# Chain products of two heads as one full tile of the matmul array, and the streams of a round called in the order of tile shapes

## The chip, the cores and the metric

The kernel runs on one core of a Trainium2 chip. Five engines run side by side: TensorE (PE in the profile, its weight loads PEld), VectorE (DVE), ScalarE (ACT), GpSimd (POOL) and SyncE (SP, which issues most DMAs). The metric is the device time of one execution in microseconds; of several executions the median counts.

## The reference

One layer of a hybrid encoder over 1024 positions and 16 learned ones, 1024 wide. A normed input goes through one projection to 5920 columns, which feed three branches; their outputs go through an output projection and are added to the input.

```
z = rms_norm(h) @ w_in
o = concat(na_branch(z), gla_branch(z), rwkv7_branch(z)) @ w_out
h = h + o ; out = rms_norm(h)[16:]

# rwkv7_branch: 8 heads of 64, two directions, a state S of 64 x 64 per head and direction
def step(S, (r, w, k, v, a, b)):
    sa = S @ a
    S  = S * w + outer(sa, b) + outer(v, k)
    y  = S @ r
```

The part that matters here is this last recurrence over the positions.

## The kernel before

All matrices with 1024 rows are split into a high and a low part (fp32r), and the projection is the sum of three products (`pj`, 24 of them per chunk of up to 512 columns). The projection is cut into jobs of 128 columns each, held in a feed.

The recurrence is computed in chunks of 64 positions. Four pairs `p` of heads, each in five groups `j` (one of a single chunk, four of four chunks per direction), make 20 units. In a pair, head e = 0 lies on partitions 0 to 63 and head e = 1 on 64 to 127. Each unit passes through these streams, which are Python generators:

- E (`early`): loads, the small products `lo` (128 rows by 128 columns of the array, written 128\*128), the running sums `Sd` (a scan on DVE) and their exponentials `E1f` and `Sd` on ACT.
- L (`late`): the products `g` inside a chunk (64\*128: 64 rows of the array, 128 columns), cut by masks into `NT`, `XR` and `GR`.
- I and J (`invert`): the inverse of a 64 x 64 triangular matrix per head, chunk and direction, by doubling, with products `fps`, `ta`, `tb`, `eps`, `cps` of 64\*64, in fp16.
- R (`rest`): transposes `v` and `t` that make `SV` and `KT`.
- C (`chain`): the recurrence itself, 68 steps, one for each chunk of each direction and pair. A step has three phases with a yield behind each. Phase 1: `c<-SV,XR` (all 128 rows, two products of 64 columns for each direction, one per head), the products `y<-XR,SV` of 64\*64, and `U` = -2 times the first result, on DVE (L848). Phase 2: `c<-U,TT` of 64\*64, copied by ACT (L853) and DVE (L854) into `SV`. Phase 3: `c<-SV,KT` and `y<-GR,SV` (128\*64 each, per head), `SV` of the next step on DVE (L862), and the output `Y` by one ACT copy (L871) or one DVE addition (L874).
- D (`drain`): the norms of finished groups, with head sums `mn` and `vr` of 128\*128.

`run` goes round these generators. In a round each is advanced once, in the order C, L, I, J, R, E, D, and then eight `pj` products are pulled from the feed. A scheduler orders the instructions of each engine by priority and by dependency afterwards, and ties the `pj` to earlier rounds by manual dependencies; each engine executes its list in order.

A product of two fp32 operands is two instructions on PE (a high and a low pass), an fp32r or fp16 product and a transpose are one. When the last unit has left R, the projection jobs that are left are pulled in one piece; then the attention and GLA branches follow, which the change doesn't touch.

Of the kernel before, what the change touches and what calls it, by code (L numbers as in the profile page):

```python
# [7 lines left out]
F32 = mybir.dt.float32  # L8
# [13 lines left out]
ALU = mybir.AluOpType  # L22

D = 1024
T = 1024
NM = 16
L = T + NM
# [3 lines left out]
C = 64  # L31
# [44 lines left out]
def emit(ctx, tc, a, out):  # L76
    nc = tc.nc
    V, S, G = nc.vector, nc.scalar, nc.gpsimd
    PS = bass.MemoryType.PSUM
    half = (slice(0, 64), slice(64, 128))  # L80
# [23 lines left out]
    PE = Tensor()  # L104
# [553 lines left out]
    def late(u, p, j):  # L658
        st = sts[u]
        ns, kn, k, r, vt, v, inc, exc, BK, dec = (st[n] for n in ("ns", "kn", "k", "r", "vt", "v", "inc", "exc", "BK", "dec4"))  # L660
        m = "" if j else "0"
        XR = it.tile([128, 2, ns, 3, C], F32, name="XR" + m, bufs=2 if j else 1)
        for e in range(2):
            es = half[e]
            (G if 0 else V).tensor_tensor(out=XR[es, :, :, 2 * e, :], in0=exc[es], in1=kn[es], op=ALU.mult)
        if j:
            (G if 1 else V).tensor_tensor(out=XR[:, :, :, 1, :], in0=r, in1=inc, op=ALU.mult)
        yield
        NT = it.tile([128, 2, ns, C], F32, name="NT" + m)
        GR = it.tile([128, 2, 2, ns, C], F32, name="GR", bufs=2) if j else None  # L670
        for d in range(2):
            gps = [mps([128, 4, 128], f"g{e}") for e in range(2)]
            nw = 128 if j else C
            for s in range(ns):
                for e in range(2):
                    es = half[e]
                    rhs = XR[es, d, s, e:e + 2, :] if j else XR[es, d, s, 2 * e, :]
                    PE.matmul(gps[e][:, s, 0:nw], lhsT=BK[es, d, s, e:e + 2, :], rhs=rhs, start=True, stop=True)
            mk = 1 if d and j else 0
            for e in range(2):  # L680
                bs, ks = half[e], half[1 - e]
                ac, rc = (C, 0) if e and j else (0, C)
                V.tensor_tensor(out=NT[bs, d], in0=gps[e][bs, 0:ns, ac:ac + C],
                                in1=nmask[bs, None, mk, :].broadcast_to([64, ns, C]), op=ALU.mult)
                V.tensor_tensor(out=XR[ks, d, :, 2 * e, :], in0=gps[e][ks, 0:ns, ac:ac + C],
                                in1=rmask[ks, None, mk, 0:C].broadcast_to([64, ns, C]), op=ALU.mult)
                if j:
                    V.tensor_tensor(out=GR[:, e, d], in0=gps[e][:, 0:ns, rc:rc + C],  # L688
                                    in1=rmask[:, None, mk, C:128].broadcast_to([128, ns, C]), op=ALU.mult)
            yield  # L690
        st.update(XR=XR, GR=GR, NT=NT)

    def rest(u, p, j):
        st = sts[u]
        ns, k, r, vt, v, BK, dec = (st[n] for n in ("ns", "k", "r", "vt", "v", "BK", "dec4"))
        m = "" if j else "0"
        for e in range(2):
            es = half[e]
            bk = BK[es, :, :, e:e + 2, :]
            G.tensor_tensor(out=bk, in0=bk, in1=dec[es, :, :, None, None].broadcast_to([64, 2, ns, 2, C]), op=ALU.mult)  # L700
        SV = it.tile([128, 2, ns, 2, C], F32, name="SV" + m, bufs=2 if j else 1)
        vps = [mps([128, 2, 4, C], f"v{e}") for e in range(2)]
        for d in range(2):
            for s in range(ns):
                i = 1 + ns * d + s
                PE.transpose(out=vps[0][:, d, s, :], in_=vt[0:64, i - 1:i + 1, :], identity=ident[0:64, 0:64])
                PE.transpose(out=vps[1][0:64, d, s, :], in_=vt[64:128, i, :], identity=ident[64:128, 64:128])
        S.copy(SV[64:128, :, :, 0, :], vps[0][64:128, :, 0:ns])
        S.copy(SV[0:64, :, :, 1, :], vps[1][0:64, :, 0:ns])
        if not j:  # L710
            for e in range(2):
                G.memset(SV[half[e], :, :, e, :], 0.0)
        st["SV"] = SV
        yield
        if j:
            if j <= 2:
                bons[p, 5 - j] = bons[p, j] = it.tile([128, 2, 256], F32, name=f"bon{j}", bufs=3 - j)
            bv = bons[p, j]
            flat = lambda t: t.rearrange("p d s c -> p d (s c)")
            if j <= 2:  # L720
                V.scalar_tensor_tensor(out=bv, in0=flat(r), scalar=hcol(28 + p), in1=flat(k), op0=ALU.mult, op1=ALU.mult)
            else:
                V.scalar_tensor_tensor(out=r, in0=r, scalar=hcol(28 + p), in1=k, op0=ALU.mult, op1=ALU.mult)
                G.tensor_tensor(out=bv, in0=bv, in1=flat(r)[:, ::-1], op=ALU.add)
                yield
                ps = head_sums("bn", bv)
                V.tensor_tensor(out=bv, in0=ps, in1=flat(v)[:, ::-1], op=ALU.mult)
                yield
        KT = it.tile([128, 2, 2, ns, C], F32, name="KT" + m, bufs=2 if j else 1)
        tps = [mps([128, 2, 4, C], f"t{e}") for e in range(2)]  # L730
        for d in range(2):
            for s in range(ns):
                for e in range(2):
                    es = half[e]
                    PE.transpose(out=tps[e][:, d, s, :], in_=BK[es, d, s, e:e + 2, :], identity=ident[es, es])
        for e in range(2):
            S.copy(KT[:, e], tps[e][:, :, 0:ns])
        st["KT"] = KT
        yield

# [71 lines left out]
    def chain(u, nu, p, j):  # L812
# [8 lines left out]
        for i in range(ns):  # L821
# [8 lines left out]
                    nx = two(sts[nu]["SV"].rearrange("p d s e c -> p (d s) e c"), 0, 4)  # L830
            cur = two(sv2, i, ns)
            dcur = two(dec, i, ns)
            cps = pq.tile([128, 3, 2, C], F32, name="c")
            for d in range(2):
                for e in range(2):
                    PE.matmul(cps[half[e], 0, d, :], lhsT=XR[:, d, sd[d], 2 * e, :], rhs=SV[:, d, sd[d], e, :], start=True, stop=True)
            if j:
                yps = pq.tile([128, 2, C], F32, name="y")
                for d in range(2):
                    for e in range(2):  # L840
                        PE.matmul(yps[half[e], d, :], lhsT=SV[half[e], d, sd[d], e, :], rhs=XR[half[e], d, sd[d], 1, :],
                                  start=not d, stop=False, skip_group_check=True)
# [6 lines left out]
            yield  # L849
            for d in range(2):  # L850
                for e in range(2):
                    PE.matmul(cps[half[e], 1, d, :], lhsT=TT[half[e], d, sd[d], :], rhs=U[half[e], d, :], start=True, stop=True)
            S.copy(cur[0:64, :, 0, :], cps[0:64, 1])  # L853
            V.tensor_copy(cur[64:128, :, 1, :], cps[64:128, 1])  # L854
            yield
            if not last:
                for d in range(2):
                    for e in range(2):
                        PE.matmul(cps[half[e], 2, d, :], lhsT=KT[:, e, d, sd[d], :], rhs=SV[:, d, sd[d], e, :], start=True, stop=True)
                for e in range(2):  # L860
                    es = half[e]
                    V.tensor_tensor(out=nx[es, :, e, :], in0=cps[es, 2], in1=dS[es], op=ALU.add)  # L862
            if j:
                for d in range(2):
                    for e in range(2):
                        PE.matmul(yps[half[e], d, :], lhsT=SV[:, d, sd[d], e, :], rhs=GR[:, e, d, sd[d], :], start=False, stop=True,
                                  skip_group_check=True)
                q0, q1 = 4 * j - 4 + i, 19 - 4 * j - i
                Yc = chunked(Y)
                if q1 > q0:  # L870
                    S.copy(Yc[:, q0:q1 + 1:q1 - q0], yps)  # L871
                else:
                    yv = Yc[:, q1:q0 + 1:q0 - q1]
                    V.tensor_tensor(out=yv, in0=yps[:, ::-1], in1=yv, op=ALU.add)  # L874
            yield

    def finish(p, j):
# [32 lines left out]
    past = []  # L910

    HPO = {}
    def run(gens, quota):
        kinds = {id(g): k for k, g in zip('CLIJRED', gens)}
        while gens:
            alive, marks = [], []
            for g in gens:
                off = HPO.get(kinds[id(g)], 0)
                if off:
                    with tc.high_priority(off):  # L920
# [4 lines left out]
                    alive.append(g)  # L925
                if seen:
                    marks.append(seen)
            gens = alive
# [630 lines left out]
```

## Time and profile before

| | before |
|---|---|
| median of 3 executions | 1480.39 us (1479.76 to 1481.89) |
| profiled execution: time | 1480.26 us |
| profiled execution: span of the core | 1478.5 us |
| PE busy | 92% of the span |
| DVE, ACT, POOL busy | 60%, 42%, 42% |
| recurrence, first `g` to last `y` | from 123.5 to 978.6 us |

The span is what the trace covers; 1.8 us lie around it. Busy time of PE is from the start of an instruction to its modelled end, and matmuls overlap, so what an instruction really takes from PE is read from the distance of one start to the next.

### The profile page before, as it was taken

Reading aid. Unit: us, or ns where it says so; the run is one execution under the profiler, and the core shown is the slowest. Engines: PE = TensorE matmul, PEld = TensorE weight load, DVE = VectorE, ACT = ScalarE, POOL = GpSimd, SP = SyncE. Lnnn points to the kernel's source line nnn. Section 1 sums busy time; section 2 is a strip of 40 time slices with the busy share of each in tenths; the row PEclk is TensorE's granted clock in tenths of the full one; section 3 lists DMA queues with packets and bytes.
Section 4 is the critical chain, followed back from the end, with each engine's and each line's share of the span. In section 5 each row is a group of like instructions: output and inputs, shape, how many; then the busy total and the mean of one; then the engine's idle time right before and its main releaser. Section 6 shows DMA issues by size and latency. Waiting matters only on the chain. (4 is left out here: it accounts for less than half of the span.)

```text
span 1478.5 us, 36082 instructions
## 1 busy us (share of the span) xinstructions
PE 1356.0 (92%) x14688; PEld 1160.2 (78%) x14688; DVE 893.9 (60%) x1952; ACT 619.0 (42%) x1400; POOL 616.0 (42%) x719
## 2 busy tenths in 40 slices
PE   5888888999899999999999999987999989789997
PEld 4887777877778788788888888776888878678786
DVE  6435455676756565756656564446767576785554
ACT  5324143334533433434334332335475645645333
POOL 6335364464636764657655554321211111210123
PEclk9998999999989999999999999998999989999999
DMA  7665543533433434333433432245342423633232
GB/s 206 143 145 132 132 107 82 129 90 73 110 102 73 120 92 115 88 103 93 107 102 80 103 94 61 64 96 146 87 130 72 127 76 103 227 111 97 95 94 92
DMA packets 184807, 158.90 MB, mean 107 GB/s; under 512 B 19152, under 2 KB 168048, under 8 KB 184640
## 3 DMA queue, kind: packets, MB, share of 16 engines
q1 hardware_dynamic: 119616, 117.12, 26.7%
q0 software_dynamic: 63264, 35.20, 13.0%
q10 hardware_dynamic: 1760, 4.26, 0.8%
q8 instruction: 116, 1.90, 0.5%
q14 instruction: 51, 0.42, 0.1%
HBM read 123.81 MB, written 32.72 MB: 106 GB/s over the span
## 5 line engine op out<-in xcount | busy, mean ns | idle before, releaser
L93 PE MATMUL pj<-hhi,whi 128*128 128x348 f32 (+10 forms) x1088 | 378.5, 348 | 9.9 <-DVE zt L263 7.5
L93 PE MATMUL pj<-hlo,whi 128*128 128x348 f32 (+10 forms) x1088 | 376.4, 346 | 0.0
L93 PE MATMUL pj<-hhi,wlo 128*128 128x348 f32 (+8 forms) x1064 | 367.6, 346 | 3.9 <-POOL wlo L166 3.9
L93 PEld LDWEIGHTS pj<-hhi,whi 128*128 128x128 f32 (+1 forms) x1088 | 212.5, 195 | 24.2 <-issue 9.7
L93 PEld LDWEIGHTS pj<-hhi,wlo 128*128 128x128 f32 x1064 | 209.5, 197 | 14.8 <-POOL wlo L166 4.4
L93 PEld LDWEIGHTS pj<-hlo,whi 128*128 128x128 f32 (+1 forms) x1088 | 212.7, 196 | 10.7 <-issue 0.7
L166 POOL TENSOR_TENSOR wlo<-wraw,whi 128x512 fp32r<-128x512 f32 x94 | 125.4, 1335 | 163.7 <-DMA whi<-in_w_in_dram 57.4
L162 POOL DMA_DIRECT2D whi<-in_w_in_dram x94 | 74.2, 790 | 144.0 <-PE pj L93 121.2
L700 POOL TENSOR_TENSOR BK<-BK,dec 64x1024 f32<-64x1024 f32 (+1 forms) x40 | 68.4, 1709 | 49.5 <-PE g L93 46.0
L846 POOL TENSOR_TENSOR dS<-SV,dec 64x128 f32<-64x128 f32 x128 | 58.9, 460 | 72.0 <-DVE SV L862 66.7
L792 ACT CAST XA<-ta 128x512 f16<-128x512 f32 (+1 forms) x92 | 49.8, 541 | 90.4 <-PE ta L93 87.1
L93 PE MATMUL ops<-hhi,oh 128*128 128x512 f32 x256 | 85.7, 401 | 2.0 <-DVE yv L1330 2.0
L786 DVE TENSOR_TENSOR Fc<-fps,im 128x512 f16<-128x512 f32 (+1 forms) x92 | 58.4, 636 | 46.5 <-PE fps L93 42.5
L93 PE MATMUL g<-XR,BK 64*128 64x128 f32 (+1 forms) x544 | 67.5, 294 | 5.8 <-DVE GR L688 5.8
L93 PEld LDWEIGHTS g<-XR,BK 64*128 64x128 f32 x544 | 53.7, 190 | 16.7 <-issue 12.5
L93 PEld LDWEIGHTS o_ps<-VC,pT 128*128 128x128 f32 (+2 forms) x384 | 53.5, 195 | 14.2 <-DVE pT L1231 7.2
L93 PE MATMUL o_ps<-VC,pT 128*128 128x64 f32 (+2 forms) x384 | 56.8, 272 | 8.0 <-DVE pT L1231 6.8
L257 ACT ACTIVATE zt<-pj,cols 128x347 f32<-128x347 f32 (+1 forms) x42 | 23.0, 549 | 85.5 <-PE pj L93 68.9
L93 PEld LDWEIGHTS ops<-hhi,oh 128*128 128x128 f32 x256 | 48.6, 191 | 13.0 <-DVE yv L1330 2.4
L1330 DVE TENSOR_TENSOR yv<-ops,yv 128x512 f32<-128x512 f32 x48 | 33.0, 688 | 42.3 <-PE ops L93 42.2
L862 DVE TENSOR_TENSOR SV<-c,dS 64x128 f32<-64x128 f32 x128 | 36.6, 286 | 34.8 <-PE c L93 32.5
L1214 ACT ACTIVATE sc<-sc,nm 128x288 f32<-128x288 f32 (+3 forms) x64 | 37.7, 588 | 45.5 <-DVE nm L1212 45.1
(302 smaller groups left out, 3039.2 us busy)
## 6 DMA issues: line engine op xcount, KB each, us to landing
whi<-in_w_in_dram POOLq DMA_DIRECT2D x94, 256.0 KB, 3.9
wraw<-in_w_in_dram SPq DMA_DIRECT2D x94, 256.0 KB
lr<-rwl POOLq DMA_DIRECT2D x32, 256.0 KB, 3.7
rwz<-zt SPq DMA_DIRECT2D x12, 544.0 KB
orr<-oscr SPq DMA_DIRECT2D x96, 64.0 KB
wr<-in_w_out_dram SPq DMA_DIRECT2D x12, 512.0 KB
glz<-zt SPq DMA_DIRECT2D x8, 544.0 KB
k<-rwz SPq DMA_DIRECT2D x32, 128.0 KB
```

The source lines that it names most:

```text
L93: return place(nc.tensor.matmul(*args, **kw))
L162: G.dma_start(out=hi, in_=w_v[:, q:q + 4, c0:c0 + 128])
L166: G.tensor_tensor(out=lo, in0=raw, in1=hi.bitcast(F32), op=ALU.subtract)
L257: S.activation(zt[:, PAD + n0:PAD + n1], ps[:, n0 - lo:n1 - lo], AF.Copy, scale=c1)
L700: G.tensor_tensor(out=bk, in0=bk, in1=dec[es, :, :, None, None].broadcast_to([64, 2, ns, 2, C]), op=ALU.mult)
L786: V.tensor_tensor(out=Fc, in0=fps, in1=mskt(l), op=ALU.mult)
L792: S.copy(A, aps)
L846: G.tensor_tensor(out=dS[es], in0=cur[es, :, e, :], in1=dcur[es, :, None].broadcast_to([64, 2, C]), op=ALU.mult)
L862: V.tensor_tensor(out=nx[es, :, e, :], in0=cps[es, 2], in1=dS[es], op=ALU.add)
L1214: S.activation(sc[:, 0:m], sc[:, 0:m], AF.Exp, bias=nm, accum_out=sm)
L1330: V.tensor_tensor(out=o, in0=ps, in1=o, op=ALU.add)
```

## The change

The two products of a direction that use all 128 rows (one per head, 64 columns each) become one product of 128 columns with both heads' 64 columns moving. Its result is 128 x 128, of which only the two diagonal blocks are read. This holds for `c<-SV,XR`, `c<-SV,KT` and `y<-GR,SV`. For that `XR` and `KT` are stored with the two heads side by side. `U` is now made in two halves, one on DVE and one on ACT (L845 and L846 of the changed kernel); `y<-XR,SV` moves from phase 1 to phase 2; `Y` is written by two copies or two additions instead of one. And the round calls its generators sorted by a rank: E 0, D 1, R 2 at its head sums, C 3 or 4 by its phase, L 5, I 6, J 7, R 8.

```diff
 late:
-            ...out=XR[es, :, :, 2 * e, :], in0=exc[es], in1=kn[es], op=ALU.mult)
+            ...out=XR[es, :, :, e, :], in0=exc[es], in1=kn[es], op=ALU.mult)
-            ...out=XR[:, :, :, 1, :], in0=r, in1=inc, op=ALU.mult)
+            ...out=XR[:, :, :, 2, :], in0=r, in1=inc, op=ALU.mult)
 rest:
+                shape["R"] = 2
                 yield
+                shape["R"] = 8
-        KT = it.tile([128, 2, 2, ns, C], F32, name="KT" + m, bufs=2 if j else 1)
+        KT = it.tile([128, 2, ns, 2, C], F32, name="KT" + m, bufs=2 if j else 1)
 chain:
-            cps = pq.tile([128, 3, 2, C], F32, name="c")
+            cps = pq.tile([128, 6, C], F32, name="c")
+            both = cps[:, 0:4].rearrange("p (d e) c -> p d e c", d=2)
+            own = cps[:, 4:6]
             for d in range(2):
-                for e in range(2):
-                    PE.matmul(cps[half[e], 0, d, :], lhsT=XR[:, d, sd[d], 2 * e, :], rhs=SV[:, d, sd[d], e, :], ...)
-            if j:
-                yps = pq.tile([128, 2, C], F32, name="y")
-                ... y<-XR,SV
+                PE.matmul(both[:, d], lhsT=XR[:, d, sd[d], 0:2, :], rhs=SV[:, d, sd[d]], start=True, stop=True)
-            V.tensor_scalar(out=U, in0=cps[:, 0], scalar1=-2.0, scalar2=None, op0=ALU.mult)
+            V.tensor_scalar(out=U[0:64], in0=both[0:64, :, 0, :], scalar1=-2.0, scalar2=None, op0=ALU.mult)
+            S.mul(U[64:128], both[64:128, :, 1, :], -2.0)
+            shape["C"] = 4
             yield
+            if j:
+                yps = pq.tile([128, 2, 2, C], F32, name="y")
+                ... y<-XR,SV
             ... c<-U,TT and its two copies
+            shape["C"] = 3
             yield
                 for d in range(2):
-                    for e in range(2):
-                        PE.matmul(cps[half[e], 2, d, :], lhsT=KT[:, e, d, sd[d], :], rhs=SV[:, d, sd[d], e, :], ...)
+                    PE.matmul(both[:, d], lhsT=KT[:, d, sd[d]], rhs=SV[:, d, sd[d]], start=True, stop=True)
             if j:
                 for d in range(2):
-                    for e in range(2):
-                        PE.matmul(yps[half[e], d, :], lhsT=SV[:, d, sd[d], e, :], rhs=GR[:, e, d, sd[d], :], ...)
+                    PE.matmul(yps[:, d], lhsT=SV[:, d, sd[d]], rhs=GR[:, :, d, sd[d], :], ...)
-                    S.copy(Yc[:, q0:q1 + 1:q1 - q0], yps)
+                    for e in range(2):
+                        S.copy(Yc[half[e], q0:q1 + 1:q1 - q0], yps[half[e], :, e, :])
 run:
+        rank = {"E": 0, "D": 1, "C": 3, "L": 5, "I": 6, "J": 7, "R": 8}
-            for g in gens:
+            for g in sorted(gens, key=lambda g: shape.get(kinds[id(g)], rank[kinds[id(g)]])):
```

How the lists of the engines change is shown at three places. The first is on PE, phase 3 of a step in pair 2 (the trace of before shows it at 641 us). Before:

```order
L93 LDWEIGHTS Fc
L93 MATMUL tb<-XU,Fc 64x64
L93 MATMUL y<-GR,SV 64x64
L93 MATMUL pj<-hhi,whi 128x346
L93 MATMUL c<-SV,KT 64x64 x4
L93 MATMUL y<-GR,SV 64x64 x3
L93 MATMUL pj<-hlo,whi 128x346
```

And the same phase of the same step in the change:

```order
L93 LDWEIGHTS Fc
L93 MATMUL tb<-XU,Fc 64x64
L93 MATMUL c<-SV,KT 128x128 x2
L93 MATMUL y<-GR,SV 128x128 x2
L93 MATMUL pj<-hlo,whi 128x346
```

Four products of `c` are two, and four of `y`, of which one stood alone ahead of a `pj`, are two behind `c`; between `tb` and the last `pj` the tile shape changes once instead of four times. The second place is on PE too, phase 1 of a later step of that pair (663 us in the trace of before; the number behind `g` is a buffer's). Before:

```order
L93 MATMUL pj<-hhi,wlo 128x342
L93 MATMUL pj<-hhi,whi 128x342
L93 MATMUL c<-SV,XR 64x64 x4
L93 MATMUL y<-XR,SV 64x64 x4
L93 MATMUL g_10070<-XR,BK 128x128
L93 MATMUL g_10071<-XR,BK 128x128
```

In the change:

```order
L93 MATMUL pj<-hhi,whi 128x342
L93 MATMUL pj<-hlo,whi 128x342
L93 MATMUL c<-SV,XR 128x128 x2
L93 MATMUL y<-XR,SV 64x64 x4
L93 MATMUL g_9910<-XR,BK 128x128
```

The `y` products still follow `c`, since the scheduler moves them up; the change of shape between `pj` and `c` is gone, those from `c` to `y` and from `y` to `g` stay. The third place is on ACT, at the exponentials of stream E for the same unit of pair 2. Before:

```order
L853 COPY SV<-c 64x2x64
L792 CAST XA<-ta 128x512
L793 CAST XU<-tb 128x512
L643 ACTIVATE E1f<-Sd 128x2x4x64
L646 ACTIVATE Sd<-Sd 128x512
L325 COPY zt<-pj 128x348
L792 CAST XA<-ta 128x512
```

In the change:

```order
L794 CAST XA<-ta 128x512
L795 CAST XU<-tb 128x512
L643 ACTIVATE E1f<-Sd 128x2x4x64
L646 ACTIVATE Sd<-Sd 128x512
L846 ACTIVATE U<-c 64x128
L325 COPY zt<-pj 128x348
L794 CAST XA<-ta 128x512
```

The new half of `U` stands on ACT right behind the exponentials, where a copy out of PSUM for the projection stood.

## Rows read from the trace of the kernel before

**Rows 1.** The page, part 1: busy time, share of the span, instructions.

```profile
PE 1356.0 (92%) x14688; PEld 1160.2 (78%) x14688; DVE 893.9 (60%) x1952; ACT 619.0 (42%) x1400; POOL 616.0 (42%) x719
```

**Rows 2.** Recurrence in windows: length, busy (count) of PE, PEld, DVE, ACT, POOL; PEclk, DMA.

```profile
123.50:300.00 176.50, 157.95 (x1919) 137.71 (x1920) 102.75 (x197) 65.47 (x143) 89.80 (x103) 0.94 0.43 108
300.00:640.00 340.00, 319.92 (x4593) 270.95 (x4593) 217.00 (x429) 136.69 (x291) 199.25 (x237) 0.94 0.39 98
640.00:880.00 240.00, 237.19 (x3597) 199.79 (x3595) 144.18 (x299) 93.62 (x205) 143.67 (x165) 1.00 0.38 97
880.00:978.60 98.60, 95.93 (x1173) 80.86 (x1173) 49.47 (x111) 30.00 (x65) 39.49 (x51) 0.98 0.28 66
sum 855.10, PE 810.99 PEld 689.32 DVE 513.41 ACT 325.78 POOL 472.20; mean PE 202.75 PEld 172.33 DVE 128.35 ACT 81.45 POOL 118.05
```

**Rows 3.** Timeline of PE, phase 1: start us, us, what, rows\*columns, form, count.

```profile
663.09 0.32 PE L93 MATMUL pj<-hhi,wlo 128*128 128x342 f32 x1
663.25 0.32 PE L93 MATMUL pj<-hhi,whi 128*128 128x342 f32 x1
663.49 0.45 PE L93 MATMUL c<-SV,XR 128*64 128x64 f32 x8
663.87 0.45 PE L93 MATMUL y<-XR,SV 64*64 64x64 f32 x8
664.25 0.49 PE L93 MATMUL g<-XR,BK 64*128 64x128 f32 x4
664.67 0.44 PE L93 MATMUL cps<-XU,Fc 64*64 64x64 f16 x16
665.04 0.42 PE L93 MATMUL pj<-hlo,whi 128*128 128x342 f32 x1
665.31 0.32 PE L93 MATMUL pj<-hhi,wlo 128*128 128x342 f32 x1
```

**Rows 4.** Timeline of PE, phase 3 of an earlier step.

```profile
640.89 0.33 PE L93 MATMUL y<-GR,SV 128*64 128x64 f32 x2
641.15 0.43 PE L93 MATMUL pj<-hhi,whi 128*128 128x346 f32 x1
641.51 0.45 PE L93 MATMUL c<-SV,KT 128*64 128x64 f32 x8
641.79 0.40 PE L93 MATMUL y<-GR,SV 128*64 128x64 f32 x6
642.12 0.43 PE L93 MATMUL pj<-hlo,whi 128*128 128x346 f32 x1
```

**Rows 5.** Timeline of PE, a longer burst of stream L.

```profile
666.49 0.94 PE L93 MATMUL g<-XR,BK 64*128 64x128 f32 x12
667.36 0.42 PE L93 MATMUL pj<-hhi,wlo 128*128 128x340 f32 x1
```

**Rows 6.** Timeline of PE in the GLA branch: products of one tile at a time.

```profile
1047.97 1.16 PE L93 MATMUL dps<-Vs,kdT 64*128 64x128 f32 x8
1049.06 0.66 PE L93 MATMUL o_ps<-VC,pT 96*128 96x64 f32 x4
```

**Rows 7.** Groups by form: count, busy us, mean ns, idle us before and releaser.

```profile
L93 PE MATMUL c<-SV,XR 128*64 128x64 f32 x544 | 32.1, 237 | 0.0
L93 PE MATMUL c<-SV,KT 128*64 128x64 f32 x512 | 32.0, 240 | 9.8 <-DVE SV L854 9.8
L93 PE MATMUL y<-GR,SV 128*64 128x64 f32 x512 | 45.1, 234 | 1.8 <-DVE SV L854 1.6 <-ACT SV L853 0.2
```

**Rows 8.** Waits of ACT: us in total, times, longest us.

```profile
ACT E1f L643 <- DVE Sd L634: 32.0, 14, 4.9
```

**Rows 9.** Instructions of single tiles: duration in ns, least, median, most.

```profile
L848 DVE TENSOR_SCALAR U<-c x68: 273/291/293, 131.6 to 974.9; 128x128 f32<-128x128 f32 x68
L871 ACT COPY Y<-y x32: 248/265/289, 227.8 to 886.7; 128x128 f32<-128x128 f32 x32
L874 DVE TENSOR_TENSOR Y<-y,Y x32: 272/291/293, 327.2 to 978.8; 128x128 f32<-128x128 f32 x32
```

More of the change, by code (lines that the diff above doesn't have):

```diff
@@ L664, in late @@
             es = half[e]
[L665 removed]
+            (G if 0 else V).tensor_tensor(out=XR[es, :, :, e, :], in0=exc[es], in1=kn[es], op=ALU.mult)
         if j:
[L667 removed]
+            (G if 1 else V).tensor_tensor(out=XR[:, :, :, 2, :], in0=r, in1=inc, op=ALU.mult)
         yield
@@ L736, in rest @@
         for e in range(2):
-            S.copy(KT[:, e], tps[e][:, :, 0:ns])
+            S.copy(KT[:, :, :, e, :], tps[e][:, :, 0:ns])
         st["KT"] = KT
@@ L847, in chain @@
             U = it.tile([128, 2, C], F32, name="U", bufs=1)
-            V.tensor_scalar(out=U, in0=cps[:, 0], scalar1=-2.0, scalar2=None, op0=ALU.mult)
+            V.tensor_scalar(out=U[0:64], in0=both[0:64, :, 0, :], scalar1=-2.0, scalar2=None, op0=ALU.mult)
+            S.mul(U[64:128], both[64:128, :, 1, :], -2.0)
+            shape["C"] = 4
             yield
+            if j:
+                yps = pq.tile([128, 2, 2, C], F32, name="y")
+                for d in range(2):
+                    for e in range(2):
+                        PE.matmul(yps[half[e], d, e, :], lhsT=SV[half[e], d, sd[d], e, :], rhs=XR[half[e], d, sd[d], 2, :],
+                                  start=not d, stop=False, skip_group_check=True)
             for d in range(2):
                 for e in range(2):
-                    PE.matmul(cps[half[e], 1, d, :], lhsT=TT[half[e], d, sd[d], :], rhs=U[half[e], d, :], start=True, stop=True)
-            S.copy(cur[0:64, :, 0, :], cps[0:64, 1])
-            V.tensor_copy(cur[64:128, :, 1, :], cps[64:128, 1])
+                    PE.matmul(own[half[e], d, :], lhsT=TT[half[e], d, sd[d], :], rhs=U[half[e], d, :], start=True, stop=True)
+            S.copy(cur[0:64, :, 0, :], own[0:64])
+            V.tensor_copy(cur[64:128, :, 1, :], own[64:128])
+            shape["C"] = 3
             yield
@@ L857, in chain @@
                 for d in range(2):
[L858 to L859 removed]
+                    PE.matmul(both[:, d], lhsT=KT[:, d, sd[d]], rhs=SV[:, d, sd[d]], start=True, stop=True)
                 for e in range(2):
                     es = half[e]
[L862 removed]
+                    V.tensor_tensor(out=nx[es, :, e, :], in0=both[es, :, e, :], in1=dS[es], op=ALU.add)
             if j:
                 for d in range(2):
[L865 to L867 removed]
+                    PE.matmul(yps[:, d], lhsT=SV[:, d, sd[d]], rhs=GR[:, :, d, sd[d], :], start=False, stop=True,
+                              skip_group_check=True)
                 q0, q1 = 4 * j - 4 + i, 19 - 4 * j - i
@@ L870, in chain @@
                 if q1 > q0:
-                    S.copy(Yc[:, q0:q1 + 1:q1 - q0], yps)
-                else:
-                    yv = Yc[:, q1:q0 + 1:q0 - q1]
-                    V.tensor_tensor(out=yv, in0=yps[:, ::-1], in1=yv, op=ALU.add)
+                    for e in range(2):
+                        S.copy(Yc[half[e], q0:q1 + 1:q1 - q0], yps[half[e], :, e, :])
+                else:
+                    for e in range(2):
+                        yv = Yc[half[e], q1:q0 + 1:q0 - q1]
+                        V.tensor_tensor(out=yv, in0=yps[half[e], ::-1, e, :], in1=yv, op=ALU.add)
             yield
@@ L927, in run @@
                     marks.append(seen)
-            gens = alive
+            gens = [g for g in gens if g in alive]
             past.append(marks)
```

11 lines of the change are left out of this document (4 added, 7 removed).

## The prediction, made blind

> **What bounds the kernel now.** I read the page first, then windows over the recurrence, then the timeline of PE inside single rounds, then the waits. The page has PE busy for 92% of the span [rows 1]. The change touches only the stretch from the first `g` to the last `y`, 855.1 us long, in which PE is busy for 811.0 us, while DVE is for 513.4 and ACT for 325.8 [rows 2]. So 44.1 us of PE's time there are idle, nearly all ahead of 640 us: in the window from 640 to 880 it is 2.8 us of 240. The granted clock follows the same line, 0.94 ahead of 640 us and 1.00 in that window [rows 2]: half of full speed (1.2 for 2.4 GHz) in a share of the time, behind stretches in which PE stood. Since all products of the stretch are executed in both versions and eight `pj` are pulled in each round, PE's list is a fixed amount of work, and the stretch takes what that list takes, plus the idle time. The question is therefore what a product costs on PE from start to start, and what a change of tile shape costs.
>
> **Prices, from starts in the timeline at full clock.** A wide product follows the next one after 0.16 us; ahead of a smaller tile it takes 0.24 (663.25 to 663.49), so leaving it costs 0.08 (elsewhere 0.09, which I use). The first wide product behind smaller tiles takes 0.27 (665.04 to 665.31), so entering costs 0.105 [rows 3]. `c<-SV,KT`, entered from a wide product and followed by its own shape, takes 0.28 for its eight instructions; the `y<-GR,SV` behind it, of the same shape and then left for a wide one, 0.33 [rows 4]. `c<-SV,XR`, entered and left, takes 0.38 [rows 3]. So leaving costs 0.10, entering 0.05, and the four products 0.232 by themselves. Eight instructions in four slots of 0.058: the two heads' products, which use different columns of the array, run two at a time.
>
> **What a full tile costs** no row of before shows exactly: fp32, 128 weight columns, 128 moving columns, all 128 rows. The nearest are two. Twelve `g` instructions (128 weight columns, 128 moving, 64 rows, two at a time) take 0.87 us, four take 0.42 [rows 3, 5]: (0.87 - 0.42) / 4 pairs = 0.112 for a slot. Eight `dps` one after the other, with the same 128 columns on both sides and no partner, take 1.09 us [rows 6]; without 0.2 for entering and leaving 0.111 each. A full tile has no partner either, and neither row depends on the number of rows, so I take 0.111 per instruction. Below it lies 0.058, if the array took 128 columns as fast as 64, which `dps` speaks against; above it 0.12.
>
> **Products.** Two products of a direction, two instructions each: 4 x 0.111 = 0.444 for a step's product, against 0.232; 0.212 more. There are 544 / 8 = 68 of `c<-SV,XR` and 512 / 8 = 64 each of the other two [rows 7], 196 in all: +41.6 us. Part of it comes back, since in the list of before the scheduler tears one product off the four in 52 of the 64 `y<-GR,SV` bursts (one head's `SV` is ready first). It then has no partner: the two instructions alone took 0.26 with entering and leaving, and the other six still 0.33 [rows 4]. That is 2 x 0.058 = 0.116 a time, 6.0 us, and 0.8 us for the other torn bursts. The changed list has almost none. Products: +34.8 us.
>
> **Shape changes.** I counted them over the built lists of PE, from the first `g` to the last `y`: 1005 before, 808 after. Priced as above (entering 64\*64 at 0.05, for fp16 bursts half of it, an estimate; entering `g` or a full `c` 0.10): gone are 177 between 128\*64 and 64\*64 (0.14 each, 24.9 us), 77 from 128\*128 to 128\*64 (0.14, 10.6), 59 back (0.205, 12.1), 42 between 128\*64 and 64\*128 (0.15, 6.4) and 14 others (2.3). New are 78 from 128\*128 to 64\*64 (0.12, 9.4), 60 back (0.20, 12.2) and 32 between 128\*128 and 64\*128 (6.1). Sum: -28.6 us. As a check, all bursts of before priced this way give 780 us; with 44 idle and 855 x 0.037 = 32 lost to the clock that is 856, against 855.1 [rows 2]. Nothing is left that could make a shape change dearer.
>
> The Trainium skill speaks on both sides here. "TensorEngine Tiling (Array Packing)", section Key Properties, says that a change of the tiling mode drains the engine, and that different tiles run in parallel. The trace agrees with both: 0.14 to 0.2 us for a change, and two heads in one slot [rows 3, 4]. By the first rule alone this change is worth some 28 us; by the second it loses what it had gained from packing, some 42.
>
> **Sum on PE:** 34.8 - 28.6 = +6.2 us at full clock, +6.4 at the stretch's mean of 0.963 [rows 2].
>
> **Other engines.** `U` in halves costs one more ACT instruction a step, by the ACT copy `Y` of 0.265 us 68 x 0.265 = 18.0 us, the DVE half as long as the whole (0.291). `Y` in halves costs 32 x 0.291 = 9.3 us of DVE and 32 x 0.265 = 8.5 of ACT [rows 9]. DVE and ACT are busy for 60% and 38% of the stretch [rows 2], so these lie beside PE; without that cover the 9.3 us of DVE would lie on the path of stream I, and I take 1 us of it. The new ACT half of `U` has a price of another kind. Behind it on PE stand the products `c<-U,TT` and all that follows them. In 6 of the 20 units it stands right behind `E1f` and its partner on ACT, where 14 `E1f` waited 32.0 us for DVE's scans [rows 8], 2.3 us each. Bounds: nothing, if the rest of the round covers it (a round is at most 855.1 / 204 = 4.2 us of PE's work), and 6 x 2.3 = 14 us if nothing does. Most is covered; I take 2 us.
>
> **Idle time.** `c<-SV,KT` waited 9.8 us, eight times, for DVE's copy of `SV` [rows 7]. With E and D called ahead of C, `lo` and head sums stand between in some rounds, which gives cover; with E's scans and sums called ahead of C, DVE's and POOL's lists could put them in front of `U` and `SV`. In the built lists of DVE they mostly stand as before. Between -10 and +10 I take 0. `y<-XR,SV` in phase 2 costs nothing: it is the same shape as `c<-U,TT`, and the scheduler moves it up anyway.
>
> The sum is 6.4 + 1 + 2 = 9.4: 1480.26 + 9.4 = 1489.7 us, so **1490**. The profiled execution is within 0.1 us of the median, so no shift between them is needed.
>
> **Rivals.** (A) The forecast, PE's list grows by more than the fewer changes give back: between +3 and +17 us, 1483 to 1497, chance 0.53. (B) Idle time falls: the recurrence ahead of 640 us has 38.6 us of idle time and a clock of 0.94 [rows 2]. Full tiles put more of PE's work between a copy and its user, and fewer pauses would also keep the clock up. If a third of the 44 goes (15 us) and 8 us of the clock's 32 with it, the sum is 9.4 - 23, 1467. It turns the sign when idle and clock together give 10 us or more. Against it: the pauses are of one to four us, behind scans and sums that stay as long. Chance 0.15. (C) The drain is what counts, as the first rule of that page has it, and the full tile is cheaper than the `g` and `dps` rows: at 0.09 an instruction the products come to +18 instead of +35 and the time to about 1473. Chance 0.05. (D) Gains and losses within 3 us of each other, 1477 to 1483: chance 0.15. (E) The ACT half of `U` is late where `E1f` waits, or the DVE additions push `Fc` and the inversion back: +14 and more on top of 6.4, 1500 to 1506; in favour speaks that ACT executes its list in order and that `E1f` waited up to 4.9 us [rows 8]. Chance 0.12. That the scheduler undoes the order is no case: the count of 808 is of its own result.
>
> A measurement of this kernel can tell about 0.2%, 3 us. From the cases: faster 0.20, same 0.15, slower 0.65. The range holds A and D and reaches into B and E until about 0.18 is outside: 1473 to 1504. The likeliest case alone is 1483 to 1497.
>
> **What would show it.** `c<-SV,XR`, `c<-SV,KT` and `y<-GR,SV` as 128\*128 with half the instructions, starting 0.11 us apart, and a phase 3 from `c` to the end of `y` of 0.9 us instead of 0.6; no 0.24 ahead of a `c` behind a wide product; the stretch from first `g` to last `y` near 865 us, the window behind 640 us with as little idle time as now, and the rest of the program as long as before. I am wrong if the full tiles start closer than 0.1 us, if the idle time of the stretch leaves 34 to 54 us, or if the clock ahead of 640 us moves by more than 0.02.

## The result and the profile after

The changed kernel takes 1500.43 us (median of 4 runs, 1499.35 to 1508.22) beside 1481.14 us of the kernel before on the same chip: a ratio of 1.0143, 95% interval 1.0111 to 1.0176. It is 1.4% slower, some 19 us where 9.4 were forecast. Its profiled execution took 1499.35 us, with a span of 1497.6.

The page of the changed kernel, part 1, answers to [rows 1]:

```profile
PE 1367.4 (91%) x13904; PEld 1189.6 (79%) x13904; DVE 913.4 (61%) x1984; ACT 646.5 (43%) x1500; POOL 618.9 (41%) x719
```

PE is busy for 11.4 us more with 784 instructions fewer. The windows of the recurrence, which answer to [rows 2], with the same columns:

```profile
122.30:300.00 177.70, 158.70 (x1853) 139.93 (x1853) 107.66 (x197) 71.75 (x164) 93.18 (x105) 0.93 0.44 107
300.00:640.00 340.00, 317.56 (x4135) 274.80 (x4134) 216.66 (x442) 141.35 (x315) 194.95 (x233) 0.95 0.39 97
640.00:880.00 240.00, 231.55 (x3172) 203.54 (x3172) 149.55 (x297) 98.79 (x230) 139.72 (x157) 0.99 0.35 91
880.00:998.00 118.00, 112.87 (x1338) 99.00 (x1336) 58.98 (x131) 40.82 (x97) 46.73 (x59) 1.00 0.28 68
sum 875.70, PE 820.68 PEld 717.26 DVE 532.85 ACT 352.71 POOL 474.58; mean PE 205.17 PEld 179.32 DVE 133.21 ACT 88.18 POOL 118.64
```

The stretch from the first `g` to the last `y` is 20.6 us longer, PE is busy for 9.7 us more of it and idle for 55.0 us instead of 44.1 (length less busy time). The window from 640 to 880 us, which had 2.8 us of idle time, has 8.5 now. The granted clock ahead of 640 us is what it was. The rest of the program behind the last `y` takes 499.7 us, as before (500.0).

Phase 1 in the timeline of PE (as [rows 3]) and phase 3 (as [rows 4]) of the changed kernel:

```profile
640.99 0.32 PE L93 MATMUL pj<-hhi,wlo 128*128 128x348 f32 x1
641.15 0.60 PE L93 MATMUL c<-SV,XR 128*128 128x128 f32 x4
641.69 0.45 PE L93 MATMUL y<-XR,SV 64*64 64x64 f32 x8
641.97 0.42 PE L93 MATMUL ta<-Fc,XU 64*64 64x64 f16 x16
...
705.89 0.42 PE L93 MATMUL tb<-XU,Fc 64*64 64x64 f16 x16
706.23 0.71 PE L93 MATMUL c<-SV,KT 128*128 128x128 f32 x4
706.78 0.61 PE L93 MATMUL y<-GR,SV 128*128 128x128 f32 x4
707.15 0.40 PE L93 MATMUL pj<-hhi,wlo 128*128 128x346 f32 x1
707.39 0.32 PE L93 MATMUL pj<-hhi,whi 128*128 128x346 f32 x1
```

A full tile follows a `pj` after 0.16 us, as one `pj` follows another, so no change is paid there. Four full tiles that are left for a smaller shape take 0.54 (641.15 to 641.69); four that are entered from one 0.55 (706.23 to 706.78). Both are four times 0.11 and a change of 0.1. From `c` to the `pj` behind `y` phase 3 takes 0.92 us, where it took 0.61 [rows 4].

The groups by form, which answer to [rows 7], and the waits of PE and ACT, of which one answers to [rows 8] (us in total, times, longest):

```profile
L93 PE MATMUL c<-SV,KT 128*128 128x128 f32 x256 | 45.3, 301 | 4.4 <-DVE SV L859 4.4
L93 PE MATMUL c<-SV,XR 128*128 128x128 f32 x272 | 45.2, 288 | 6.0 <-DVE SV L867 5.8
L93 PE MATMUL y<-GR,SV 128*128 128x128 f32 x256 | 41.5, 286 | 1.4 <-DVE SV L859 1.4
```

```profile
ACT U L846 <- DVE U L845: 85.3, 42, 10.2
ACT E1f L643 <- DVE Sd L634: 26.0, 15, 3.6
PE ta L93 <- DVE Fc L788: 16.1, 14, 3.2
PE c L93 <- ACT U L846: 1.9, 3, 0.9
```

In the kernel before, the wait of `ta` and a wait of DVE on ACT were:

```profile
PE ta L93 <- DVE Fc L786: 5.3, 9, 2.4
DVE SV L854 <- ACT SV L853: 28.2, 19, 3.5
```

The wait of `c<-SV,KT` for DVE's copy has halved (9.8 us before), but `ta` waits 16.1 us for `Fc`, and a new wait of 85.3 us stands on ACT: its half of `U` waits for DVE's half. PE itself waits for that half only 1.9 us. The kernel before has the same kind of pair already: DVE's copy of one half of `c` into `SV` waited 28.2 us for ACT's copy of the other half. The single tiles, as in [rows 9]:

```profile
L845 DVE TENSOR_SCALAR U<-c x68: 255/283/284, 130.6 to 994.6; 64x128 f32<-64x128 f32 x68
L846 ACT ACTIVATE U<-c x68: 259/273/275, 133.0 to 995.6; 64x128 f32<-64x128 f32 x68
L876 ACT COPY Y<-y x64: 242/261/277, 223.0 to 903.7; 64x128 f32<-64x128 f32 x64
```

A half takes nearly as long as a whole did (0.283 us beside 0.291 for `U` on DVE, 0.261 beside 0.265 for `Y` on ACT).

### The profile page after: what moved, and what is told of

Read it like the earlier page. It is cut to its first block, busy times and chain, and to the rows that moved or that the text cites. A ratio compares the mean times of both kernels' runs of the same rounds, so it can differ in the third digit from the quotient of the medians.

```text
span 1497.6 us, 34706 instructions
## 1 busy us (share of the span) xinstructions
PE 1367.4 (91%) x13904; PEld 1189.6 (79%) x13904; DVE 913.4 (61%) x1984; ACT 646.5 (43%) x1500; POOL 618.9 (41%) x719
## 4 chain that ended last, share of the span: by engine, by line
PE 61%; DVE 16%; DMA 8%; ACT 7%; issue 5%; POOL 2%; SPq 1%; DVEq 0%; POOLq 0%; ACTq 0%
PE pj L93 26%; PE ops L93 8%; PE c L93 5%; PE g L93 3%; PE y L93 3%; PE o_ps L93 2%; DMA rb<-rscr 2%; PE ta L93 1%; DVE Sd L634 1%; PE fps L93 1%; DVE SP L1158 1%; DVE GB L1092 1%; PE tps L96 1%; DVE XR L665 1%; PE t L96 1%
## 5 line engine op out<-in xcount | busy, mean ns | idle before, releaser
L93 PEld LDWEIGHTS pj<-hlo,whi 128*128 128x128 f32 (+1 forms) x1088 | 212.4, 195 | 10.1 <-issue 1.0
L93 PEld LDWEIGHTS pj<-hhi,wlo 128*128 128x128 f32 x1064 | 208.7, 196 | 12.5 <-POOL wlo L166 4.5
L843 POOL TENSOR_TENSOR dS<-SV,dec 64x128 f32<-64x128 f32 x128 | 56.1, 438 | 65.7 <-DVE SV L867 60.1
L867 DVE TENSOR_TENSOR SV<-c,dS 64x128 f32<-64x128 f32 x128 | 36.8, 287 | 44.1 <-PE c L93 41.6
```

Of the source, the lines that this page charges most:

```text
L93: return place(nc.tensor.matmul(*args, **kw))
L867: V.tensor_tensor(out=nx[es, :, e, :], in0=both[es, :, e, :], in1=dS[es], op=ALU.add)
```

## The experiments

For each run the table has the ratio to the kernel before on the same chip with its interval, and then three numbers of the stretch in the one execution that was profiled (with products per head, `y` in phase 2 and `y` in phase 1 this was the fastest, 5 to 9 us below the median). Idle is the sum of PE's gaps of more than 0.15 us; PE's list is the length of the stretch less this idle time and less half of the time at 1.2 GHz, so it is PE's work at full clock; and the fourth is the wait of `ta` for `Fc`. The last column comes from all executions again: each has the mean granted clock of its whole span, and the span times what is missing of the clock is the most that the clock can have cost. It is a mean, good to 1 to 4 us; that of the kernel before on the same chip stands in parentheses, where it is on record.

| kernel | ratio (95%) | idle, us | PE's list, us | `ta` for `Fc`, us | clock, us |
|---|---|---|---|---|---|
| before | 1 | 43.6 | 779.0 | 5.3 | 63.5 to 66.3 |
| before, a second profile | - | 42.3 | 779.8 | 6.8 | - |
| changed | 1.0143 (1.0111 to 1.0176) | 53.7 | 791.1 | 16.1 | 66.0 |
| changed, both halves of `U` on DVE | 1.0127 (1.0102 to 1.0151) | 58.0 | 791.9 | 14.5 | 59.9 (65.7) |
| changed, old order | 1.0104 (1.0075 to 1.0134) | 55.1 | 790.0 | 11.7 | 63.5 (65.7) |
| changed, products per head | 1.0049 (1.0026 to 1.0071) | 59.9 | 777.8 | 18.3 | 64.0 (65.7) |
| changed, `y` in phase 1 | 1.0162 (1.0122 to 1.0203) | 53.4 | 790.4 | 19.9 | 63.5 (66.3) |
| changed, old order and `y` in phase 1 | 1.0045 (1.0023 to 1.0068) | 50.0 | 789.3 | 9.3 | 56.4 (65.6) |
| before, `U` in halves | 1.0038 (1.0009 to 1.0068) | 45.6 | 782.7 | 8.2 | 61.9 (65.7) |
| before, `Y` in halves | 0.9940 (0.9916 to 0.9965) | 45.2 | 781.0 | 6.3 | 54.6 (63.5) |
| before, `y` in phase 2 | 1.0050 (1.0029 to 1.0071) | 58.1 | 775.5 | 10.1 | 62.6 (63.5) |
| before, new order | 0.9992 (0.9968 to 1.0015) | 44.5 | 780.6 | 15.9 | 60.2 (63.5) |
| before, `y<-GR` behind `c<-SV,KT` | 0.9974 (0.9951 to 0.9997) | 51.1 | 764.0 | 8.8 | 63.3 (63.5) |
| the last one and `Y` in halves | 0.9903 (0.9874 to 0.9932) | 51.0 | 767.6 | 8.3 | 56.9 (66.3) |

**The second profile of before** (no edit) sets the scale.

> The kernel before once more, unchanged, with a profile of its own, as a measure of what one profile differs from another. If the idle time of the stretch is 41 to 47 us and PE's list 777 to 782 us, then idle times of 54 to 60 us in the other profiles are outside of what chance gives; if it lies between 47 and 55, the idle times of single profiles tell nothing.

Two profiles of one kernel differ by 1.3 us of idle time and 0.8 us of list; as far as two can tell, the 50 to 60 us of other profiles are not chance. The part of the program behind the stretch, the same work in all kernels, took between 493.7 and 502.0 us over the profiles (500.0 and 495.9 in the two of before), so a single span tells less than the numbers of the table. Half of the clock's cost lies outside of the stretch too: ahead of it and behind it together it was 24 to 36 us in these profiles (33.1 and 27.4 in the two of before). The ratio of a whole kernel has that in it.

**Both halves of `U` on DVE**, in the changed kernel: is it the ACT half that makes the idle time?

```diff
-            S.mul(U[64:128], both[64:128, :, 1, :], -2.0)
+            V.tensor_scalar(out=U[64:128], in0=both[64:128, :, 1, :], scalar1=-2.0, scalar2=None, op0=ALU.mult)
```

> The changed kernel, but both halves of U are made on DVE, so that ACT has no half of U and no wait for DVE's half (85.3 us, 42 times in the changed kernel). Theory 1, the new idle time comes from that wait: the idle time of PE in the recurrence falls from 53.7 us back to about 44 and the time from 1500 to about 1490. Theory 2, the loss is all in PE's own list (full tiles of 0.11 us an instruction): the time stays at 1498 to 1502. The list as priced from rows changes by -3 us only.

The time did not change by more than the intervals (1.0127 beside 1.0143), and the idle time did not fall (58.0). ACT's wait of 85 us is gone with its instruction, and nothing came of it: it is not where the 10 us come from.

**The old order** in the changed kernel:

```diff
-            for g in sorted(gens, key=lambda g: shape.get(kinds[id(g)], rank[kinds[id(g)]])):
+            for g in gens:
```

> The changed kernel with the streams of a round called in the old order. The built list of PE has 802 changes of tile shape against 808 with the new order and 1005 before. Theory A, the fewer shape changes come from the full tiles alone and the order does nothing behind the scheduler: 1498 to 1503. Theory B, the order saves time or costs it by moving DVE and ACT work of the streams E and D ahead of the chain: more than 5 us away from the changed kernel on either side.

PE's list is 790.0 us, no longer than with the new order. The built list (the order in which the scheduler gives PE its instructions) has 802 changes of tile shape without the order and 808 with it: all of the fewer changes come from the full tiles. The time is 5.8 us below that of the changed kernel, which the intervals do not set apart, so the theories stay undecided here.

**Products per head** in the changed kernel: `c` and `y` again as 64-column products of one head each, written into the diagonal blocks; order, halves and the moved `y` stay.

```diff
-                PE.matmul(both[:, d], lhsT=XR[:, d, sd[d], 0:2, :], rhs=SV[:, d, sd[d]], start=True, stop=True)
+                for e in range(2):
+                    PE.matmul(both[half[e], d, e], lhsT=XR[:, d, sd[d], e, :], rhs=SV[:, d, sd[d], e, :], start=True, stop=True)
...
```

> The changed kernel, but with one product per head and direction of 64 columns instead of the full tile, written to the diagonal blocks alone; order, halves of U and of Y as in the change. The list as priced loses 33 us of products and gains 24 us of shape changes (976 of them): -9 us. Theory 1 (PE's list and the wait for the half of U share the loss): about 1490, half of the way back, with idle time of the recurrence still above 50 us. Theory 2 (all of it is the full tile): about 1481. Theory 3 (all of it is the halves of U): 1500.

The list falls by 13.3 us to that of before, and the ratio by 0.0094, some 14 us. So this is what full tiles cost here. The idle time doesn't fall (59.9): it belongs to what was left in. Theory 1 has the kind right, with more of the way back than half.

**`U` in halves**, alone in the kernel before:

```diff
-            V.tensor_scalar(out=U, in0=cps[:, 0], scalar1=-2.0, scalar2=None, op0=ALU.mult)
+            V.tensor_scalar(out=U[0:64], in0=cps[0:64, 0], scalar1=-2.0, scalar2=None, op0=ALU.mult)
+            S.mul(U[64:128], cps[64:128, 0], -2.0)
```

> The kernel before with one edit: U in two halves, the upper one on ACT. Theory 1: ACT waits for DVE's half here too, some 80 us in 40 waits, PE's idle time in the recurrence rises by 5 to 12 us and the time from 1481 to 1486 to 1493. Theory 2 (the wait is hidden by the rest of the round): 1480 to 1483.

It costs 0.38%, 5.6 us. From the waits of that kernel:

```profile
ACT U L849 <- DVE U L848: 73.7, 41, 6.9
```

ACT's half waits for DVE's: in none of the 68 steps does it start before DVE's half has ended, so what was one instruction ahead of `c<-U,TT` is two in a row. But PE waits for ACT's half only once in this run:

```profile
PE c L93 <- ACT U L849: 0.3, 1, 0.3
```

So by PE's waits the two in a row are not what costs 5.6 us. In the one profile PE's list is 3.7 us longer and the idle time 2.0; why is not shown. Theory 1 is right about ACT's wait and the time, and wrong about the idle time.

**`Y` in halves**, alone in the kernel before:

```diff
-                    S.copy(Yc[:, q0:q1 + 1:q1 - q0], yps)
+                    for e in range(2):
+                        S.copy(Yc[half[e], q0:q1 + 1:q1 - q0], yps[half[e]])
... (the addition on DVE likewise)
```

> The kernel before with only the output Y written in two halves (two ACT copies or two DVE additions instead of one); products, U and order as before. Theory 1 (the added 9 us of DVE work make Fc late, and the 10 us of added idle time come from here): idle of the stretch 51 to 56 us, the wait of ta for Fc 10 us or more instead of 5.3, 6 to 10 us slower. Theory 2 (the added instructions are hidden, the idle time comes from the y products moved to phase 2 or from the order): idle 42 to 47 us, within 3 us of before. The built list is priced at 780.6 us, as before (779.9).

Hardly any idle time is added (45.2 us beside 43.6 and 42.3), and it is faster by 0.6%, which neither theory had. In its profile the granted clock from 300 to 500 us is higher than in both profiles of before. The windows, with PE's busy time, granted clock and DMA, of the kernel with `Y` in halves:

```profile
300.00:400.00 100.00, 92.07 (x1381) 0.98 0.39 98
400.00:500.00 100.00, 94.17 (x1422) 0.98 0.43 106
```

and of the kernel before:

```profile
300.00:400.00 100.00, 92.30 (x1334) 0.95 0.39 98
400.00:500.00 100.00, 94.35 (x1362) 0.91 0.41 103
```

PE spent 51.2 us of the stretch at 1.2 GHz instead of 64.8, which is 6.8 us at full speed. Over all executions the clock of the whole span cost at most 54.6 us, beside 63.5 in the kernel before on that chip: 8.9 us less, as much as the gain. But in the profile the stretch is only 3.2 us shorter (851.9 beside 855.1); the other 6.7 us of the span lie ahead of it and behind it, in work that the edit does not touch. Why the clock held, there and in the stretch, is not settled, and how much of the 0.6% the halves themselves make is not shown.

**`y` in phase 2**, alone in the kernel before (the four `y<-XR,SV` moved behind the first yield, ahead of `c<-U,TT`):

```diff
-            if j:
-                yps = ...   # y<-XR,SV
             ... U
             yield
+            if j:
+                yps = ...   # y<-XR,SV
             for d in range(2):  # c<-U,TT
```

> The kernel before with only y<-XR,SV moved from phase 1 behind the first yield, ahead of c<-U,TT. The built list of PE has 971 shape changes instead of 1005 and is priced at 776.0 us instead of 779.9. Theory 1 (idle time comes from DVE's additions): idle as before, 42 to 47 us, 2 to 5 us faster, 1476 to 1479 beside 1480.4. Theory 2 (with y behind the yield less of PE's work covers the wait for U, and the 10 us of idle time come from here): idle 51 to 56 us, 4 to 8 us slower.

The list became 3.5 us shorter, as priced, and the kernel 0.5% slower: the idle time rose by 14.5 us. The waits of PE in that kernel:

```profile
PE ta L93 <- DVE Fc L786: 10.1, 10, 3.3
PE c L93 <- DVE SV L854: 8.2, 7, 2.2
PE xps L96 <- DVE XU L772: 6.1, 7, 1.7
PE c L93 <- DVE SV L862: 4.3, 5, 2.3
PE y L93 <- ACT SV L853: 3.0, 2, 2.6
```

It is spread over many waits, and no one of them has it all. In the built list `y<-XR,SV` stands right behind `c<-SV,XR` in 54 steps before, and in 35 now; elsewhere it is placed behind a `pj` or in front of `c<-U,TT`. In the trace of the changed kernel it is 32, so that its `y` products still follow `c` holds for half of the steps. The scheduler does not move them all the way back.

**The new order**, alone in the kernel before:

```diff
+        rank = ...   # and the lines that set shape["R"] and shape["C"]
-            for g in gens:
+            for g in sorted(gens, key=lambda g: shape.get(kinds[id(g)], rank[kinds[id(g)]])):
```

> The kernel before, with the round's generators called in the changed kernel's rank order and nothing else. Theory 1 (the order by itself does nothing on PE: the built list still has 1005 shape changes, as before, and is priced at 777.9 us against 779.9): within 3 us of the kernel before, idle time of the stretch 40 to 48 us. Theory 2 (the order is what delays DVE's products for the inversion and so makes the 10 us of added idle time): idle 52 to 56 us and 6 to 10 us slower.

The time is that of before, and so is the sum of the idle time; but the waits change places:

```profile
PE ta L93 <- DVE Fc L788: 15.9, 11, 2.7
PE c L93 <- DVE SV L866: 1.7, 2, 1.6
PE c L93 <- DVE SV L857: 1.3, 3, 0.6
```

`c<-SV,KT` waits 1.3 us for the copy of `SV` instead of 9.8 [rows 7], and `ta` 15.9 instead of 5.3. In all kernels with the new order `ta` waits 14.5 to 19.9 us, in all others 5.3 to 11.7. What `Fc` stands behind is seen on DVE in the changed kernel, here with PE's timeline of the same microseconds:

```profile
406.54 0.28 DVE L845 TENSOR_SCALAR U<-c 64x128 f32<-64x128 f32 x1
406.75 3.13 DVE L665 TENSOR_TENSOR XR<-E1f,kn 64x512 f32<-64x512 f32 x2
409.92 0.69 DVE L788 TENSOR_TENSOR Fc<-fps,im 128x512 f16<-128x512 f32 x1
```

```profile
410.66 0.44 PE L93 MATMUL ta<-Fc,XU 64*64 64x64 f16 x16 [2.57 <-DVE Fc L788]
```

Stream L's two multiplications `XR` hold DVE for 3.1 us. At the same place of the kernel before (402.77 to 406.12) they do so as well, but there it is the copy of `SV` that comes late for PE. At this place the block on DVE is the same, and what differs is the product that waits behind it.

**`y` back in phase 1** in the changed kernel (the diff of `y` in phase 2, reversed), and then also **the old order** (its diff above):

> The changed kernel with y<-XR,SV put back into phase 1, right behind c<-SV,XR; full tiles, order, halves of U and Y stay. Theory 1 (the moved y is what adds the 10 us of idle time): idle of the stretch 42 to 48 us instead of 53.7, and since the built list is priced 3.8 us longer than the changed kernel's (790.2 against 786.4), 4 to 8 us faster than the changed kernel: a ratio to the kernel before of 1.008 to 1.011 instead of 1.0143. Theory 2 (the added idle time is that of the full tiles or of all the parts together): idle 52 to 60 us and a ratio of 1.014 to 1.018.

> Full tiles with nothing of the rest of the change but what they need: U and Y in halves; y<-XR,SV in phase 1 and the generators in the order of before. Neither half brought idle time by itself (45.6 and 45.2 us). The built list is priced at 787.8 us. Theory 1 (the full tiles themselves bring idle time, since each product of the chain ends 0.2 us later and DVE, which waits for it, comes later to the inversion's products): idle of the stretch 50 to 57 us and a ratio of 1.012 to 1.017. Theory 2 (it takes the new order or the moved y beside the full tiles): idle 42 to 48 us and a ratio of 1.006 to 1.010. PE's list in both 789 to 793 us.

Of the first, theory 1 falls: the idle time stays (53.4), and the ratio is not below that of the changed kernel. Of the second, the idle time is 50.0, at the lower end of theory 1, and the time below what either had: the full tiles with only the halves that they need cost 0.45%, 6.6 us. In the stretch they cost more: in the profile it is 14.9 us longer, with 10.3 us of list and 6.4 of idle time, and 1.7 less for the clock, while the work ahead of it and behind it lost 6.9 us less to the clock than in the first profile of before, though 1.2 less than in the second (26.2, 33.1 and 27.4 us). Over all runs the clock of the whole span cost less as well, 56.4 us beside 65.6. The two kernels differ by the order alone, and their intervals are apart: with full tiles, the order that cost nothing before costs 0.0117, 17 us. The waits of the second:

```profile
PE ta L93 <- DVE Fc L788: 9.3, 6, 2.8
PE c L93 <- ACT U L852: 7.0, 4, 4.6
```

and of the first:

```profile
PE ta L93 <- DVE Fc L788: 19.9, 16, 3.2
PE c L93 <- ACT U L852: 2.4, 3, 1.1
```

The wait of `ta` is 10.6 us longer with the order, others are shorter. The two profiles differ by 3.4 us of idle time and 1.1 us of list. Over all runs some 6 us of the 17, good to 4, go with the clock of the whole span (2.8 us less than before with the order, 9.2 less without). In the stretch of the two profiles it is the same, 61.4 us at 1.2 GHz, so this part is not shown to come from the products of the stretch. The remainder no profile shows.

**The four `y<-GR,SV` held together** behind `c<-SV,KT`, in the kernel before, without full tiles:

```diff
-                        PE.matmul(cps[half[e], 2, d, :], lhsT=KT[:, e, d, sd[d], :], ...)
+                        tied = PE.matmul(cps[half[e], 2, d, :], lhsT=KT[:, e, d, sd[d], :], ...)
...
-                        PE.matmul(yps[half[e], d, :], lhsT=SV[:, d, sd[d], e, :], rhs=GR[:, e, d, sd[d], :], ...)
+                        r = PE.matmul(yps[half[e], d, :], lhsT=SV[:, d, sd[d], e, :], rhs=GR[:, e, d, sd[d], :], ...)
+                        if not last:
+                            tc.add_manual_dep(r.ins, tied.ins.name, NOSYNC, reason="issue order")
```

> The kernel before with one thing added: the scheduler is told to place the four y<-GR,SV of a step behind its last c<-SV,KT, so that no product is torn off the four and put in front of a projection product. Two heads still run side by side in 64 columns. The built list has 947 shape changes instead of 1005 and is priced at 763.4 us instead of 779.9. Theory 1 (the list of PE at my prices is what the time follows): 10 to 16 us faster, 1464 to 1470 beside 1480.4, list 763 to 767. Theory 2 (the torn-off product was free since PE waited for the other head's SV there): the list falls, but c<-SV,KT or y<-GR,SV then wait 8 us more for the copies of SV; within 5 us of before.

The group of `y<-GR,SV` in its trace:

```profile
L93 PE MATMUL y<-GR,SV 128*64 128x64 f32 x512 | 29.6, 229 | 1.9 <-DVE SV L854 1.9
```

The same 512 instructions are busy for 29.6 us instead of 45.1 [rows 7], and PE's list is 15.0 us shorter, where 16.5 were priced. Of this 3.9 us arrive (ratio 0.9974). In the profile idle time takes 7.5 and 3.5 go to the clock (71.7 us at 1.2 GHz instead of 64.8), but over all runs the clock cost as much as before (63.3 and 63.5 us), so that what took the other 3.6 us is not settled. Theory 1 is right about the list, theory 2 about the time, though the wait of `c` for `SV` did not grow (9.1 us).

**With `Y` in halves beside it:**

> The kernel before with its 64-column products, y<-GR,SV placed behind c<-SV,KT, and Y written in halves: the two parts that were faster alone (ratios 0.9974 and 0.9940). List priced at 766.0 us. Theory 1 (the two gains are independent, one on PE's list and one beside it): ratio 0.989 to 0.993, some 11 to 16 us faster than before. Theory 2 (what a shorter list gives goes into idle time, as idle rose from 44 to 51 us with the tied y alone): ratio 0.994 to 0.998, idle over 50 us.

1463.57 us (11 runs, 1457.72 to 1477.67) beside 1480.78: 0.97% faster, and the best version found. The two ratios hold together (their product is 0.9914), and the clock stays up as with `Y` in halves alone (51.2 us at 1.2 GHz in the profile, 56.9 beside 66.3 us over all runs).

## Why the prediction was right in direction and too low

**The full tile's price was right.** 0.111 us was taken from `g` and `dps`; full tiles follow each other after 0.112, and a change to or from a smaller shape costs 0.1. "TensorEngine Tiling (Array Packing)" of the Trainium skill, section Key Properties, says that different tiles run in parallel. The runs agree: the full tile, which gives that up for half the instructions, has a list 13.3 us longer than the same kernel with products per head.

**What the shape changes give back was sized too high.** The list grew by 12.1 us, not 6.2. I summed the distances from start to start by kind, at full clock and without idle time, in both traces (12.5 us in all). The chain's 128-row products with their exits took 17.2 us more and `pj` 3.9 us less, together +13.3; the prices over the built lists had made it +13.8. What is missing lies in the others: transposes, `g`, head sums and 64\*64 products should have given 7.1 us back (13.8 - 7.1 is the forecast's 6 to 7) and gave 0.8. That the priced sum of before agreed with its trace to a microsecond did not show this: by the same sums the transposes were priced 6 us too high there and the fp16 products 4 too low, and the two hid each other. How the priced sum splits by kind is worked out over the built lists, and no trace shows it.

**The idle time was the other half.** It was taken to change by nothing, within 10 us, and rose by 10.1. By the prediction's own measure, length less busy time, it is 55.0 us and outside of the 34 to 54 that it gave as a sign of being wrong; the stretch is 875.7 us, where it wanted about 865. One step that failed is "`y<-XR,SV` in phase 2 costs nothing: it is the same shape as `c<-U,TT`, and the scheduler moves it up anyway". That move alone added 14.5 us of idle time and 0.5%. It is not the whole answer, since with full tiles and the new order moving it back gained nothing. The two edits don't add up: each of them costs when it is made without the other beside full tiles (+0.59% for the move, +1.17% for the order, over 1.0045), and both together cost +0.98%. The clock may be a part of that: the full tiles with their halves alone lost 56.4 us to it over the span, with either edit 63.5 and with both 66.0, so that most goes with the first of the two. The profiles of the stretch do not show it, and the cause stays open.

**"That the scheduler undoes the order is no case" was wrong in its reason.** 808 was the count of the whole change; the order by itself leaves it at 1005. On PE the order gave nothing. It moved PE's wait for DVE from `SV` to `Fc`, both of which the text had named, one as a gain and the other as a loss; alone they cancel.

**The halves.** For the ACT half of `U` 2 us were taken, between 0 and 14, because of `E1f`; 5.6 us (1.3 to 10) were measured in the kernel before. Neither `E1f` nor ACT's place behind DVE explains them, since PE waited for that half 0.3 us there. In the changed kernel it waited 1.9 us, near the 2 that were taken, but of these three waits one, 0.45 us, came behind `E1f`. The cause of the 5.6 us is open. `Y` in halves was put at +1 us, and the kernel with it was 8.9 us faster, as much as the clock of the span cost less; the sum had no term for the clock.

**Rivals.** A's mechanism came about, with a sum beyond its end (19 us, where 17 was the most). The time is E's, 1500 to 1506, and the longest wait is the one that E's second half named, `ta` behind a late `Fc`; but the DVE additions that E blamed for it added hardly any idle time alone (45.2 us), and neither did the ACT half of `U` (45.6). That the time lies within the stated 1473 to 1504 is therefore in part luck: the range reached that far for E's sake, and E's causes are not what the runs show. B had the opposite sign: more work of PE in the chain did not cover the waits. C falls with 0.112 a slot.

What stays open: which dependency turns the moved `y` and the order into idle time (it is spread over many short waits), why both are not additive, and why the kernel with `Y` in halves loses less to the clock.

## What to carry to other kernels

Before two half-width products are fused into one full tile to save instructions and shape changes, ask whether they run side by side already: then the array's columns are in use, the full tile takes twice the time (here 0.112 us beside 0.058), and only some of the shape changes come back. Where a scheduler tears a burst of small products apart, hold the burst together first: that removed more of PE's list here (15 us) at no price in columns. And a list that is priced right in sum is not priced right in its parts; compare kind by kind with the trace before differences are taken from it. Where one profile shows another clock, look at the clock of all runs, and at the work that no edit touched, before it is put into the account.

## What the runs showed that was not expected

- Two engines that read different halves of one PSUM tile did not run side by side: ACT's half of `U` waited for DVE's 42 times in 68, 85.3 us in all, and never started before it had ended. The wait is for a semaphore that DVE's half raises; the trace does not show what demands it. The copies of `SV` show the same in the kernel before, 28.2 us, where it could have been read ahead of the prediction.
- A shorter list of PE comes back only in part: 15.0 us of work removed gave 3.9 us of time, and 7.5 went to idle time in the profile.
- One and the same order of calls cost nothing with 64-column products (0.9992) and 17 us with full tiles and `y` in phase 1, of which some 6 go with the clock of the whole span.
- With `Y` in halves the clock cost 8.9 us less over 11 runs, and 6.7 us of the profile's gain lie outside of the stretch that the edit touches.
